# A two-head recurrence on one core: products on half tiles of the matrix array turned into whole-array products

## The chip, the cores and the metric

One core of a Trainium2 chip runs the kernel. The time is device microseconds (us) of one execution; lower is better. A run of a kernel gives one time, and a profiled execution gives the trace from which all rows below are taken. Five engines work side by side, each on a stream of its own: PE (the 128x128 matrix array, with PEld for its weight loads), DVE (vector), ACT (scalar), POOL (GpSimd) and SP (which issues most DMAs). "Fill" is used below for matrix work that depends on no other work at hand.

## The reference, cut to what matters

Two batches of 512 tokens go through one layer: an RWKV-7 branch run in both directions, an attention branch (MLA), gates, an output projection, then a feed-forward block. The change is in the RWKV-7 branch. Per head (8 of them, 64 channels) and direction the recurrence is

```python
def step(state, inp):
    r_t, w_t, k_t, v_t, kk_t, a_t = inp
    sa = jnp.einsum('bhvk,bhk->bhv', state, kk_t)
    state = (state * w_t[:, :, None, :]
             - sa[..., None] * (kk_t * a_t)[:, :, None, :]
             + v_t[..., None] * k_t[:, :, None, :])
    return state, jnp.einsum('bhvk,bhk->bhv', state, r_t)
```

## The kernel before, in words

**Units, chunks and products.** The recurrence is computed in chunks of 64 tokens (`CH`), eight per sequence (`NCH`). A unit is one batch and one pair of heads (4 pairs, 2 batches, 8 units, named `00`, `10`, `01`, ... for batch and pair); head A lies on partitions 0 to 63 (`HA`), head B on 64 to 127 (`HB`), and the two directions are `i` or `d` = 0, 1. `state()` goes through the chunks of one unit. For each chunk PE does, for both directions and both heads:

- s1 (L892, L893): reads the state; K = 128, 64 columns, once into `HA` and once into `HB`. DVE copies the result to `rs` (L895).
- o1 (L904, L906): the part of the output that reads the state, into the bank `o`.
- s2 (L917, L918): the solve, the inverse matrix `e` of the chunk times `rs`; K = 64, one product per head. ACT copies head A's half into `sva` (L919), DVE head B's into `svb` (L920).
- s3 (L925, L926): what the chunk adds to the state; K = 128. DVE adds it to the decayed state `sp` (L927, L928; `sp` is made by POOL, L913, L914).
- o inner (L930, L932): the part of the output inside the chunk, `arb` times `sva`/`svb`; K = 64.

A product of plain f32 appears in the trace as two records, each with a weight load. The shapes in the rows (`128*64`, `64*64`, `128*128`) are the rows and columns of the array that a record uses. All s1, s2 and s3 results share one PSUM buffer (`st`, `NST` = 1).

**Around the recurrence.** `prep()` makes a unit's operands (products `gx`, `gy`; DVE masks them into `nt`, `arb`, `kra`, `krb`; transposes `tb`, `tk`, `vp`, copied out by ACT through `tr_halves`, L641). `lanes()` inverts the 32x32 diagonal blocks on POOL, through DRAM (`nt_d`, `e_d`). `merge()` loads the inverses into `e` (L863), transposes a block (L864, tile `tp`) and joins the blocks by small products `zp` and `xp`. `post()` normalises the output of a unit.

**What sets the order.** Six generators (state, post, merge, prep, fill, combine) are run by `drive()`, which keeps a planned time per thread: a `yield L1` says how much planned time must pass before the thread goes on, and threads are taken in the order of that list. PE instructions keep exactly the order in which `drive()` meets them; the instructions of the other engines are placed by a scheduler. The fill thread supplies the projections `pj_rkv`, `pj_gt`, later the attention (`sc`, `pt`, `pav`, `qps`, `kps`). Those projections are products of 128x128 by 512 in a rounded f32 format. The numbers `L1`, `L2`, `L3` (recurrence), `YT2` (prep's transposes), `YO1` (post) and `YQ` (attention) are such planned times.

Of the kernel before, what the change touches and what calls it, by code (L numbers as in the profile page):

```python
# [41 lines left out]
L1 = 0.7  # L42
L2 = 0.9
L3 = 1.0
# [17 lines left out]
YT2 = 0.8  # L62
YM1 = 2
YM2 = 1.1
YO1 = 1.3
# [3 lines left out]
YQ = 2.6  # L69
# [35 lines left out]
def trunk(ctx, tc, outs, x, w_in, w2, g2, w_uq, w_ukk, w_ukv, w_oab, w_out, w_gu, w_down,  # L105
# [524 lines left out]
    NI = 2  # L630
    HA, HB = slice(0, 64), slice(64, 128)
# [54 lines left out]
    class Unit:  # L686
        count = 0
        first = True

        def __init__(self, b, p):  # L690
            self.b, self.p, self.nm = b, p, f"{b}{p}"
            self.par = Unit.count % 2
            Unit.count += 1
# [4 lines left out]
        def prep(self, free):  # L698
            b, p, nm, tmp = self.b, self.p, self.nm, self.tmp
            kra, krb, arb, bka, bkb = [], [], [], [], []  # L700
# [47 lines left out]
            sva = rp.tile([P, NI, NCH, CH], F32, tag="sva", bufs=2, name=f"sva{nm}")  # L748
            svb = rp.tile([P, NI, NCH, CH], F32, tag="svb", bufs=2, name=f"svb{nm}")
# [4 lines left out]
            for d, (rev, pp_, bt_, kt_) in enumerate(halves):  # L754
# [7 lines left out]
                nt_ = rp.tile([P, NCH, CH], F32, tag="nt", bufs=1, name=f"nt{nm}{d}")  # L762
                rb_ = rp.tile([P, NCH, CH], F32, tag="arb", bufs=4, name=f"arb{nm}{d}")
                for g in range(2):
# [8 lines left out]
                    nc.vector.tensor_mul(nt_[:, gs], gx[:, :, 0:CH], mb[:, :, 0:CH])  # L773
                    nc.vector.tensor_mul(rb_[:, gs], gx[:, :, CH:], mb[:, :, CH:])
                for h, hs in enumerate((HA, HB)):
                    q0 = (d * 2 + h) * NCH
                    nc.sync.dma_start(nt_d[self.par][q0:q0 + NCH].rearrange("c r t -> r c t"), nt_[hs])
# [3 lines left out]
            for d, (rev, pp_, bt_, kt_) in enumerate(halves):  # L781
# [12 lines left out]
                ba_ = rp.tile([P, NCH, CH], F32, tag="bka", bufs=4, name=f"bka{nm}{d}")  # L794
                bb_ = rp.tile([P, NCH, CH], F32, tag="bkb", bufs=4, name=f"bkb{nm}{d}")
# [14 lines left out]
                bka.append(ba_), bkb.append(bb_)  # L810
            self.sva, self.svb, self.pc = sva, svb, pc
            self.kra, self.krb, self.arb, self.bka, self.bkb = kra, krb, arb, bka, bkb

        def lanes(self):
# [15 lines left out]
            for s in range(31):  # L830
                n = 31 - s
                for eng, m0, m1, el in els:
# [3 lines left out]
                    lt = rp.tile([P, 144], F32, tag=f"lt{m0}", bufs=1, name=f"lt{nm}{s}{m0}")  # L836
# [13 lines left out]
        def merge(self):  # L850
# [3 lines left out]
            for i in range(NI):  # L854
                e_ = rp.tile([P, NCH, CH], F32, tag="e", bufs=4, name=f"e{nm}{i}")

                def tmp3(name):
                    return rp.tile([P, NCH, 32], F32, tag=name, bufs=1, name=f"{name}{nm}{i}")
                tp, ntl, z_ = tmp3("tp"), tmp3("ntl"), tmp3("z")
                for h, hs in enumerate((HA, HB)):  # L860
                    q = slice((i * 2 + h) * NCH, (i * 2 + h + 1) * NCH)
                    nc.sync.dma_start(ntl[Q[2 * h]], nt[q, 0:32, 32:].rearrange("c r t -> r c t"))
                    nc.sync.dma_start(e_[hs], ed[q].rearrange("c r t -> r c t"))  # L863
                nc.vector.transpose(tp, e_[:, :, 0:32])  # L864
# [8 lines left out]
                for c in range(NCH):  # L873
                    for h in range(2):
                        mm(xp_[Q[2 * h], c], z_[Q[2 * h + 1], c], e_[Q[2 * h + 1], c, 32:],
                           tile_position=(h * 64 + 32, h * 64))
                yield YM2
                for h in range(2):
                    (nc.scalar.copy, nc.vector.tensor_copy)[h](e_[Q[2 * h], :, 32:], xp_[Q[2 * h], 0:NCH])
                self.ee.append(e_)  # L880

        def state(self):
            nm, sva, svb, pc, ee = self.nm, self.sva, self.svb, self.pc, self.ee
            kra, krb, arb, bka, bkb = self.kra, self.krb, self.arb, self.bka, self.bkb
# [3 lines left out]
               skip_group_check=True)  # L888
            for c in range(NCH):
                s1 = psf.tile([P, NI, CH], F32, tag="st", bufs=NST, name=f"s1{nm}{c}")  # L890
                for i in range(NI):
                    mm(s1[HA, i], kra[i][:, c, 0:CH], sva[:, i, c])  # L892
                    mm(s1[HB, i], krb[i][:, c, 0:CH], svb[:, i, c])  # L893
                rs_ = rp.tile([P, NI, CH], F32, tag="rs", bufs=3, name=f"rs{nm}{c}")
                nc.vector.tensor_copy(rs_, s1)  # L895

                def oslice(i):
                    cn = c if i == 0 else NCH - 1 - c
                    return slice(cn * CH, (cn + 1) * CH)

                def orev(i, t):
                    return t if i == 0 else t[:, ::-1]
                for i in range(NI):
                    mm(op[HA, oslice(i)], sva[:, i, c], orev(i, kra[i][:, c, CH:]), start=False, stop=False,  # L904
                       skip_group_check=True)
                    mm(op[HB, oslice(i)], svb[:, i, c], orev(i, krb[i][:, c, CH:]), start=False, stop=False,  # L906
                       skip_group_check=True)
                last = c == NCH - 1
                yield L1
                if not last:  # L910
                    sp_ = rp.tile([P, NI, CH], F32, tag="rs", bufs=3, name=f"sp{nm}{c}")
# [3 lines left out]
                s2 = psf.tile([P, NI, CH], F32, tag="st", bufs=NST, name=f"s2{nm}{c}")  # L915
# [3 lines left out]
                nc.scalar.copy(sva[HA, :, c], s2[HA])  # L919
                nc.vector.tensor_copy(svb[HB, :, c], s2[HB])  # L920
                yield L2
                if not last:
                    s3 = psf.tile([P, NI, CH], F32, tag="st", bufs=NST, name=f"s3{nm}{c}")
# [3 lines left out]
                    nc.vector.tensor_add(sva[HA, :, c + 1], s3[HA], sp_[HA])  # L927
# [785 lines left out]
```

## Time and profile before

| what | value |
|---|---|
| three runs | 1833.29, 1835.57, 1837.47 us; median 1835.57 |
| the profiled execution | 1835.74 us, span of the trace 1834.0 us |
| mean granted PE clock | 0.978 |
| recurrence (first s1 to last s1) | 278 to 897 us |
| PE, DVE, ACT, POOL busy | 95%, 61%, 42%, 35% of the span |

How to read it: a unit's eight chunks take about 50 us, some 80 us pass from one unit's first chunk to the next one's. Between the chunks' products PE runs fill. A PE record's length is longer than its distance to the next record, since records overlap; so costs on PE are read from starts, not from lengths.

### The profile page before, as it was taken

How to read it: one execution, taken by the hardware profiler on the slowest of the kernel's cores; microseconds unless marked ns; L12 is line 12 of the kernel's file. 1: busy time of each engine (PE TensorE's matmuls, PEld its weight loads, DVE VectorE, ACT ScalarE, POOL GpSimd, SP SyncE). 2: the span in 40 equal slices, each digit the busy share in tenths (PEclk: the TensorE clock that was granted, in tenths of full speed). 3: DMA queues.
4: the chain of work that ended last, by engine and by line, in shares of the span. 5: the costliest groups of instructions: out<-in, count | busy, mean ns of one | idle time of the engine just before them, and what ended most of it. 6: DMA issues, size and time to landing. Idle time of an engine off the chain costs nothing.

```text
span 1834.0 us, 31000 instructions
## 1 busy us (share of the span) xinstructions
PE 1734.3 (95%) x11676; PEld 1365.7 (74%) x11676; DVE 1116.9 (61%) x1957; ACT 771.0 (42%) x1496; POOL 642.2 (35%) x992
## 2 busy tenths in 40 slices
PE   6999999999999998899989999699999999989997
PEld 6887766777677775565657979578888888868886
DVE  6633555635364455877786556865655555588757
ACT  5434343333434334656663233333333333335445
POOL 3012345362635536161112123853434333100006
PEclk8999989999999998999999999899999999999999
DMA  4354433425343334212067551022222222274342
GB/s 163 123 175 163 123 107 82 124 71 136 81 125 106 89 113 119 61 36 55 21 233 249 190 178 35 24 81 93 103 95 84 92 81 92 98 273 134 121 139 92
DMA packets 185333, 208.97 MB, mean 114 GB/s; under 512 B 102816, under 2 KB 114464, under 8 KB 185184
## 3 DMA queue, kind: packets, MB, share of 16 engines
q1 hardware_dynamic: 184320, 205.48, 35.4%
q8 instruction: 92, 1.51, 0.3%
q10 hardware_dynamic: 720, 0.98, 0.2%
q0 software_dynamic: 144, 0.52, 0.1%
q14 instruction: 57, 0.47, 0.1%
HBM read 147.70 MB, written 59.24 MB: 113 GB/s over the span
## 4 chain that ended last, share of the span: by engine, by line
PE 70%; DVE 9%; DMA 8%; POOL 5%; issue 3%; ACT 2%; SPq 1%; DVEq 0%; POOLq 0%; ACTq 0%
PE pgC L125 9%; PE pj_gt L125 8%; PE pgB L125 6%; PE pgA L125 6%; PE pj_rkv L125 5%; PE dx L125 5%; PE dy L125 3%; PE s L125 3%; PE pab L125 2%; PE sc L125 2%; PE pav L125 2%; PE pj_mla L125 2%; DMA wor<-in_w_out 2%; PE o L125 2%; PE gx L125 2%
## 5 line engine op out<-in xcount | busy, mean ns | idle before, releaser
L839 POOL TENSOR_TENSOR lt<-lane,el 128x126 f32<-128x126 f32 (+22 forms) x248 | 93.4, 377 | 38.1 <-DMA lane<-nt_d 19.6
L841 POOL TENSOR_TENSOR el<-el,lt 128x126 f32<-128x126 f32 (+22 forms) x248 | 98.6, 398 | 19.0
L125 PE MATMUL pab<-yo,wab 128*128 128x512 f32 x384 | 94.7, 400 | 5.9 <-ACT yo L132 3.2
L125 PE MATMUL pj_gt<-h_hi,whi_gt 128*128 128x512 f32 x240 | 99.2, 413 | 0.0
L125 PE MATMUL pj_gt<-h_hi,wlo_gt 128*128 128x512 f32 x240 | 98.8, 412 | 0.1
L125 PE MATMUL pj_gt<-h_lo,whi_gt 128*128 128x512 f32 x240 | 98.1, 409 | 0.0
L125 PE MATMUL pwo<-woh,m 128*128 128x256 f32 x512 | 93.8, 283 | 0.1
L125 PEld LDWEIGHTS pab<-yo,wab 128*128 128x128 f32 x384 | 71.9, 191 | 26.0 <-DVE wab L133 4.2
L1203 POOL TENSOR_TENSOR s<-uraw 128x512 f32<-128x512 f32 x22 | 29.3, 1330 | 152.1 <-DMA uraw<-in_w_gu 152.1
L125 PEld LDWEIGHTS pwo<-woh,m 128*128 128x128 f32 x512 | 80.3, 192 | 0.6 <-ACT woh L132 0.3
L125 PE MATMUL pj_rkv<-h_hi,wlo_rkv 128*128 128x512 f32 x192 | 79.7, 418 | 0.0
L125 PE MATMUL pj_rkv<-h_lo,whi_rkv 128*128 128x512 f32 x192 | 79.1, 412 | 0.0
L125 PE MATMUL pj_rkv<-h_hi,whi_rkv 128*128 128x512 f32 x192 | 78.3, 408 | 0.0
L125 PE MATMUL pwo<-wol,m 128*128 128x256 f32 x256 | 72.4, 284 | 0.9 <-DVE wol L133 0.9
L1582 POOL TENSOR_TENSOR x<-x,dp 128x512 f32<-128x512 f32 x4 | 6.3, 1590 | 178.1 <-DVE x L1581 178.1
L1271 DVE TENSOR_TENSOR p<-p,pgC 128x512 f32<-128x512 f32 x22 | 15.1, 687 | 86.9 <-PE pgC L125 86.9
L919 ACT COPY sva<-s 64x128 f32<-64x128 f32 x64 | 16.5, 258 | 104.6 <-PE s L125 96.3
L1050 POOL TENSOR_TENSOR g<-g 128x512 f32<-128x512 f32 x16 | 24.9, 1554 | 92.7 <-DVE g L1048 84.5
L466 POOL TENSOR_SCALAR lut<-lut 128x512 f32<-128x512 f32 x32 | 20.5, 641 | 98.4 <-ACT lut L464 98.1
L125 PEld LDWEIGHTS pj_gt<-h_hi,wlo_gt 128*128 128x128 f32 x240 | 45.1, 188 | 9.5 <-DVE wlo_gt L133 0.8
L125 PEld LDWEIGHTS pj_gt<-h_hi,whi_gt 128*128 128x128 f32 x240 | 45.1, 188 | 8.6
L125 PEld LDWEIGHTS pj_gt<-h_lo,whi_gt 128*128 128x128 f32 x240 | 45.1, 188 | 8.4
(1559 smaller groups left out, 5552.9 us busy)
## 6 DMA issues: line engine op xcount, KB each, us to landing
graw<-in_w_gu SPq DMA_DIRECT2D x22, 512.0 KB, 3.5
uraw<-in_w_gu SPq DMA_DIRECT2D x22, 512.0 KB, 3.5
a_d<-a SPq DMA_DIRECT2D x21, 512.0 KB, 3.3
w<-in_w_down SPq DMA_DIRECT2D x42, 256.0 KB, 4.1
x<-in_x SPq DMA_DIRECT2D x16, 512.0 KB, 8.2
rwkv_in<-lut SPq DMA_DIRECT2D x32, 256.0 KB, 2.0
gate_d<-gtt SPq DMA_DIRECT2D x32, 256.0 KB, 2.5
wab<-in_w_oab SPq DMA_DIRECT2D x32, 256.0 KB, 3.6
```

What stands on the lines that cost most here:

```text
L125: pin(nc.tensor.matmul(out, lhsT, rhs, start=start, stop=stop, **kw), n if out.shape[0] > 64 else n / 2)
L466: nc.gpsimd.tensor_scalar(t, t, f, f, op0=ALU.mult, op1=ALU.add)
L839: eng.tensor_mul(lv, lane[:, s, s + 1:].unsqueeze(1).to_broadcast([P, m_, n]), el[:, 0:m_, s].unsqueeze(2).to_broadcast([P, m_, n]))
L841: eng.tensor_add(ev, ev, lv)
L919: nc.scalar.copy(sva[HA, :, c], s2[HA])
L1050: nc.gpsimd.tensor_add(g_[:, 0], g_[:, 0], g_[:, 1])
L1203: vg(ES[min(j, 1)]).tensor_add(s1, a21, a22)
L1271: nc.vector.tensor_add(p1, p1, x_)
L1582: nc.gpsimd.tensor_add(xs(1, t, 1), xs(1, t, 1), p5[t])
```

## The change

Three things are done to the recurrence.

1. **Solve and state addition on the whole array.** `e` becomes a tile of 128 columns that holds both heads' inverses as two diagonal blocks, zero elsewhere (zeroed once by POOL). One product of K = 128 per direction replaces the two of s2. `bka`/`bkb` become one tile `bk`, `sva`/`svb` halves of one tile `sv`, and s3 is one product 128x128x128 per direction, of whose result only the two diagonal blocks are read.
2. **The inner output product of a chunk moves** from behind that chunk's s3 to behind the next chunk's o1 (`o_inner(c - 1)`); the last chunk's stays where it was.
3. **Room in SBUF**: three `e` tiles (`NEB`) instead of four, which also serve as `nt`; `merge()`'s second direction therefore waits until the state of the unit before is done, since it overwrites that unit's first `e`; `tp` and `z` share a buffer; `rs` has two buffers, not three; `lanes()` writes its intermediate into used rows of `lane`. The mask product into `nt` and the transposes are issued per head (two instructions for one), since the two heads' blocks no longer lie in the same columns.

Five planned times change with it: `L1` 0.7 to 0.57, `L3` 1.0 to 1.06, `YT2` 0.8 to 0.93, `YO1` 1.3 to 1.02, `YQ` 2.6 to 2.89.

```diff
...
+            if not Unit.e:
+                Unit.e = [rp.tile([P, NCH, P], F32, name=f"e{j}") for j in range(NEB)]
+                for t in Unit.e:
+                    for h, hs in enumerate((HA, HB)):
+                        nc.gpsimd.memset(t[hs, :, (1 - h) * CH:(2 - h) * CH], 0.0)
...
-                    nc.vector.tensor_mul(nt_[:, gs], gx[:, :, 0:CH], mb[:, :, 0:CH])
+                    for h, hs in enumerate((HA, HB)):
+                        nc.vector.tensor_mul(nt_[h][:, gs], gx[hs, :, 0:CH], mb[hs, :, 0:CH])
...
+                if i and self.at and NEB < 4:
+                    yield has("state", self.at - 1)
+                e_ = Unit.e[(2 * self.at + i) % NEB]
...
-                nc.vector.transpose(tp, e_[:, :, 0:32])
+                    nc.vector.transpose(tp[Q[2 * h]], eh(h, 0, Q[2 * h]))
...
+                if c:
+                    o_inner(c - 1)
...
                 for i in range(NI):
-                    mm(s2[HA, i], ee[i][HA, c], rs_[HA, i])
-                    mm(s2[HB, i], ee[i][HB, c], rs_[HB, i])
...
+                    mm(s2[:, i, 0:CH], ee[i][:, c], rs_[:, i])
...
                     for i in range(NI):
-                        mm(s3[HA, i], bka[i][:, c], sva[:, i, c])
-                        mm(s3[HB, i], bkb[i][:, c], svb[:, i, c])
...
+                        mm(s3[:, i], bk[i][:, c], sv[:, i, c])
...
-                for i in range(NI):
-                    mm(op[HA, oslice(i)], sva[HA, i, c], orev(i, arb[i][HA, c]), start=False,
-                       stop=False, skip_group_check=True)
-                    mm(op[HB, oslice(i)], svb[HB, i, c], orev(i, arb[i][HB, c]), start=False,
-                       stop=False, skip_group_check=True)
+                if last:
+                    o_inner(c)
                 yield L3
```

How the built program's order changes is shown at three places of unit `02`, the fifth of the eight. In the names, digits behind s1, s2, s3 are the unit and the chunk (`s3023` is s3 of unit 02, chunk 3), and the number behind the underscore is the buffer.

**First place, PE, chunk 3.** Before, s3 and the inner output products of the same chunk stand together, ahead of the gate projection `pj_gt`:

```order
L125 MATMUL s3023_6800<-sva02_5347,bka020_5741 64x64 [waits DVE_49]
L125 MATMUL s3023_6800<-svb02_5348,bkb020_5742 64x64
L125 MATMUL s3023_6800<-sva02_5347,bka021_5915 64x64
L125 MATMUL s3023_6800<-svb02_5348,bkb021_5916 64x64
L125 MATMUL o02_6435<-arb020_5456,sva02_5347 64x64
L125 MATMUL o02_6435<-arb020_5456,svb02_5348 64x64
L125 MATMUL o02_6435<-arb021_5531,sva02_5347 64x64
L125 MATMUL o02_6435<-arb021_5531,svb02_5348 64x64
L125 MATMUL pj_gt600_6817<-h_hi0_137,whi_gt600_6821 128x512
```

Now the chunk begins with s1, o1 and then the inner output products of chunk 2 (the rows with `arb`):

```order
L125 MATMUL s1023_6415<-sv02_5160,kra020_5164 64x64 [waits DVE_49,PE_49]
L125 MATMUL s1023_6415<-sv02_5160,krb020_5165 64x64
L125 MATMUL s1023_6415<-sv02_5160,kra021_5296 64x64
L125 MATMUL s1023_6415<-sv02_5160,krb021_5297 64x64
L125 MATMUL o02_6140<-kra020_5164,sv02_5160 64x64
L125 MATMUL o02_6140<-krb020_5165,sv02_5160 64x64
L125 MATMUL o02_6140<-kra021_5296,sv02_5160 64x64
L125 MATMUL o02_6140<-krb021_5297,sv02_5160 64x64
L125 MATMUL o02_6140<-arb020_5248,sv02_5160 64x64 x2
L125 MATMUL o02_6140<-arb021_5320,sv02_5160 64x64 x2
```

and its s3 is two whole-array products between the prep's transposes `tk` and the projection:

```order
L129 MATMUL tk120_6453<-idn_62,kt120_6045 128x128 x3
L125 MATMUL s3023_6462<-sv02_5160,bk020_5494 128x128 [waits DVE_49]
L125 MATMUL s3023_6462<-sv02_5160,bk021_5670 128x128
L125 MATMUL pj_gt511_6118<-h_hi1_139,whi_gt511_6127 128x512
L125 MATMUL pj_gt511_6118<-h_lo1_140,whi_gt511_6127 128x512
```

Four half-tile products became two whole-array ones, and the half-tile inner products now stand beside other half-tile products.

**Second place, PE, chunk 0.** Before, the solve s2 follows directly on prep's products `gx` of the next unit, which use the array in the same 64x64 tiles:

```order
L125 MATMUL gx1201_6450<-kra120_6321,bt120_6293 64x128
L125 MATMUL gx1201_6450<-krb120_6322,bt120_6293 64x128
L125 MATMUL s2020_6462<-rs020_6442,e020_6210 64x64 [waits DVE_49]
L125 MATMUL s2020_6462<-rs020_6442,e020_6210 64x64
L125 MATMUL s2020_6462<-rs020_6442,e021_6334 64x64 x2
L125 MATMUL pj_gt510_6399<-h_hi0_137,whi_gt510_6403 128x512
```

Now `gx` stands ahead of a whole-array s2:

```order
L125 MATMUL gx1200_6154<-kra120_6069,bt120_6042 64x128
L125 MATMUL gx1200_6154<-krb120_6070,bt120_6042 64x128
L125 MATMUL s2020_6166<-rs020_6147,e2_1715 128x64 [waits DVE_49]
L125 MATMUL s2020_6166<-rs020_6147,e0_1713 128x64 [waits Activation_49]
L125 MATMUL pj_gt510_6117<-h_lo0_138,whi_gt510_6121 128x512
```

The pair keeps its place, but its two groups no longer share a tile shape.

**Third place, ACT, chunk 3.** Before, ACT copies out the transposes `tb` and `tk` of the next unit's prep and makes `kt` for the unit after it, and only then copies the solve's result:

```order
L641 COPY bka120_6710<-tk120_6766 64x4x64 [waits PE_49]
L641 COPY bka120_6710<-tk120_6766 64x4x64
L641 COPY bkb120_6711<-tk120_6766 64x4x64 x2
L743 ACTIVATE kt030_7265<-a030_7255,oka_66,col_60 128x512 [waits DMAHW1_49]
L919 COPY sva02_5347<-s2023_6780 64x2x64 [waits PE_49,Pool_49]
```

Now the copy stands ahead of those of `tk` and of `kt`:

```order
L642 COPY bk120_6399<-tb120_6430 64x4x64 x3
L940 COPY sv02_5160<-s2023_6444 64x2x64 [waits PE_49,Pool_49]
L642 COPY bk120_6399<-tk120_6453 64x4x64 [waits PE_49]
L642 COPY bk120_6399<-tk120_6453 64x4x64 x3
L746 ACTIVATE kt030_6950<-a030_6940,oka_66,col_60 128x512 [waits DMAHW0_49]
```

Five instructions that stood ahead of the copy now stand behind it.

More of the change, by code (lines that the diff above doesn't have):

```diff
@@ L809, in prep @@
                 yield YT2
[L810 to L812 removed]
+                bk.append(bk_)
+            self.sv, self.pc = sv, pc
+            self.kra, self.krb, self.arb, self.bk = kra, krb, arb, bk
         def lanes(self):
```

92 lines of the change are left out of this document (51 added, 41 removed).

## The prediction

> **What bounds the kernel now.** I read the page first, then the busy time by stretches, then the waits of PE inside the recurrence, then the timeline of PE around single products.
>
> ```profile
> span 1834.0 us, 31000 instructions
> ...
> PE 1734.3 (95%) x11676; PEld 1365.7 (74%) x11676; DVE 1116.9 (61%) x1957; ACT 771.0 (42%) x1496; POOL 642.2 (35%) x992
> ```
>
> ```profile
> 600.00:680.00 80.00, 78.97 (x823) 59.06 (x820) 38.26 (x82) 30.73 (x66) 41.24 (x93) 1.00 0.37 103
> ```
>
> ```profile
> PE s L125 <- DVE svb L920: 14.5, 13, 2.8
> ...
> PE s L125 <- DVE rs L895: 2.9, 4, 1.0
> ```
>
> PE is busy 1734.3 of 1834.0 us. The second fence is one unit's 80 us (columns: length, then PE, PEld, DVE, ACT, POOL busy, granted clock, DMA share, GB/s): PE has work for 78.97 of 80 us at full clock, since fill stands between the chunks' products. The recurrence's latency is therefore hidden, and a microsecond counts only if PE spends it in the array or waits. The third fence lists what PE waited for between 278 and 905 us (total, times, longest): 14.5 us for the solve's result ahead of s3, 2.9 us for `rs` ahead of s2. So the change is worth what it saves of array time, plus what it does to these waits.
>
> **Array time: the price of a half-tile group.** What a group costs is the distance between the fill around it, less the fill's own pitch.
>
> ```profile
> 613.91 0.40 PE L125 MATMUL pj_gt<-h_hi,whi_gt 128*128 128x512 f32 x1
> 614.14 0.39 PE L125 MATMUL pj_gt<-h_lo,whi_gt 128*128 128x512 f32 x1
> 614.49 0.45 PE L125 MATMUL s<-rs,e 64*64 64x64 f32 x8
> 614.87 0.50 PE L125 MATMUL pj_gt<-h_hi,wlo_gt 128*128 128x512 f32 x1
> 615.20 0.40 PE L125 MATMUL pj_gt<-h_hi,whi_gt 128*128 128x512 f32 x1
> ```
>
> ```profile
> 625.76 0.22 PE L125 MATMUL s<-sva,kra 128*64 128x64 f32 x1
> ...
> 626.11 0.22 PE L125 MATMUL o<-kra,sva 128*64 128x64 f32 x1
> ...
> 629.66 0.40 PE L125 MATMUL pj_gt<-h_hi,wlo_gt 128*128 128x512 f32 x1
> ...
> 630.23 0.22 PE L125 MATMUL s<-sva,bka 128*64 128x64 f32 x1
> 630.29 0.22 PE L125 MATMUL s<-sva,bka 128*64 128x64 f32 x1
> ...
> 630.45 0.27 PE L125 MATMUL o<-arb,sva 64*64 64x64 f32 x1
> ...
> 630.56 0.22 PE L125 MATMUL o<-arb,sva 64*64 64x64 f32 x1
> ...
> 630.83 0.50 PE L125 MATMUL pj_gt<-h_hi,whi_gt 128*128 128x512 f32 x1
> 631.17 0.40 PE L125 MATMUL pj_gt<-h_lo,whi_gt 128*128 128x512 f32 x1
> ```
>
> Fill starts every 0.23 us (613.91 to 614.14). From 614.14 to 615.20 lie 1.06 us; two pitches of fill taken off leave 0.60 us for s2. Inside a group a pair of records, one per head, takes 0.058 us (six pairs from 625.76 to 626.11, s1 and o1 of one chunk). s2's eight records are four pairs, 0.23 us, so going from whole-array fill into half tiles and back costs 0.60 - 0.23 = 0.37; fill's starts scatter by 0.01, and I use 0.36. Between two half-tile groups of different shape (s3, then o) the last pair is followed after 0.16 us (630.29 to 630.45) and o's first pair after 0.11 (to 630.56): 0.15 more than two pairs, less than half of an in-and-out.
>
> **Array time: the price of a whole-array group.** The trace has no whole-array f32 product of 64 or 128 columns. Its nearest rows are the f32 products `ss_kk` (whole array, 2 columns) and the f32 transposes `tb` (whole array, 128 columns):
>
> ```profile
> 244.08 0.40 PE L125 MATMUL pj_rkv<-h_lo,whi_rkv 128*128 128x512 f32 x1
> 244.32 0.95 PE L125 MATMUL ss_kk<-blk2sb,kksq 128*128 128x2 f32 x8
> 245.13 0.48 PE L125 MATMUL pj_rkv<-h_hi,wlo_rkv 128*128 128x512 f32 x1
> 245.45 0.40 PE L125 MATMUL pj_rkv<-h_hi,whi_rkv 128*128 128x512 f32 x1
> ```
>
> ```profile
> 215.47 0.39 PE L125 MATMUL pj_rkv<-h_lo,whi_rkv 128*128 128x512 f32 x1
> 215.70 0.60 PE L129 MATMUL tb<-idn,bt 128*128 128x128 f32 x4
> 216.05 0.47 PE L125 MATMUL pj_rkv<-h_hi,wlo_rkv 128*128 128x512 f32 x1
> 216.37 0.39 PE L125 MATMUL pj_rkv<-h_hi,whi_rkv 128*128 128x512 f32 x1
> ```
>
> By the same measure eight records of `ss_kk` cost 1.37 - 0.46 = 0.91 us, 0.114 each, and four of `tb` 0.90 - 0.46 = 0.44, 0.110 each, with no price for entering or leaving. That both agree at 2 and at 128 columns says that the weights' load sets the pitch; I take 0.110, the row nearest to s3's 128 columns. From below it can hardly be less; from above it is 0.110 + 0.107 if a record's load and its two passes of 128 columns do not overlap (0.107 is twice 128 of the 512 columns that fill streams in 0.23, less its overhead).
>
> **The sum of the array time.** s2 and s3 are 64 and 56 steps of eight half-tile records, 480 pairs at 0.058 = 27.8 us. They become 120 steps of four whole-array records, 480 at 0.110 = 52.8 us: 25.0 us more. Against that stand the changes of tile shape, which I counted in the two built orders: between whole array and part of it 456 before, 320 now, so 68 fewer in-and-outs at 0.36 = 24.5 us less; between half-tile shapes 108 before, 78 now, 30 at 0.15 = 4.5 less. The sum is 25.0 - 29.0 = -4.0 us. Taken alone a chunk between fill would save more: s2 0.60 to 0.44, s3 with o 1.05 (629.66 to 631.17 less two pitches) to 0.44 + 0.38 for o, together some 0.4. It doesn't come to that, because many groups have prep's half-tile products as neighbours:
>
> ```profile
> 626.83 0.40 PE L125 MATMUL pj_gt<-h_hi,wlo_gt 128*128 128x512 f32 x1
> 627.16 0.32 PE L125 MATMUL gy<-kra,kt 64*64 64x128 f32 x1
> ...
> 628.02 0.45 PE L125 MATMUL s<-rs,e 64*64 64x64 f32 x8
> 628.40 0.50 PE L125 MATMUL pj_gt<-h_hi,whi_gt 128*128 128x512 f32 x1
> 628.73 0.39 PE L125 MATMUL pj_gt<-h_lo,whi_gt 128*128 128x512 f32 x1
> ```
>
> `gy` runs from 627.16 to 628.02 and s2 follows in the same tiles, so the two share one in-and-out: there s2 costs only its four pairs, 0.23 us, and on the whole array 0.44. In the built orders 21 of 64 s2 stood so before and 22 stand so now; s1, which gains from such a neighbour too, had one 21 times and has it 9 times.
>
> The Trainium skill, page "TensorEngine Tiling (Array Packing)", section "Theoretical Speedup", speaks against this change: a product whose rows or columns fit 64 gains up to two times by half tiles, so giving them up would double the groups, to 27.8 us more. The rows bear that out (0.110 against 0.058). Its section "Key Properties" has the other half, that a change of tiling mode drains the array; by the first rule alone the sum would be 1835.7 + 27.8 = 1863.5 us, by both it is near the one above. The first alone gets no chance of its own: the rows from 614.14 to 615.20 show the in-and-out's price, and the change removes 68 of them.
>
> **The waits.** Four of them change.
>
> ```profile
> 621.42 0.82 ACT L743 ACTIVATE kt<-a,oka,col 128x512 f32<-128x512 f32 x1
> 622.27 0.26 ACT L919 COPY sva<-s 64x128 f32<-64x128 f32 x1
> ...
> 622.98 0.27 PE L125 MATMUL s<-sva,bka 128*64 128x64 f32 x1 [0.59 <-DVE svb L920]
> ```
>
> - Ahead of s3: in chunk 3 of five units ACT makes `kt` (0.82 us) before it copies the solve's result, and PE waits, here 0.59 us. The changed order puts the copy first in four of these five: about -3 us with the longest of them. The fill between s2 and s3 stays six products, but s2 no longer leaves half tiles, so s3 comes some 0.2 us sooner after its input; for the 13 waits that is +2.6. Net -0.4.
> - Ahead of s2: o inner now lies between s1 and s2 and gives 0.38 us (630.45 to 630.83) of cover; L1 is shorter, but fill there falls by about one product at most. DVE's `rs` copy stood behind a mask product of `gx` in 13 chunks and does so in 2. I take -2.5 of the 2.9 us.
> - Ahead of the next s1: the same 0.38 us of cover is gone between s3 and s1, with six fill products left (1.38 us). Two DVE additions of 0.28 and 0.295 us follow s3 and have to end; 1.38 covers them unless DVE is busy. I take +1.5; the bounds are 0 and 56 x 0.38 = 21.
> - In `merge()`: two transposes instead of one, and the second direction's wait for the first one's `xp`, because `tp` and `z` share a buffer. I take +0.5, bounded by 8 x 0.44 x 2 = 7.
>
> Together -0.9 us.
>
> **The rest.**
>
> ```profile
> L773 DVE TENSOR_TENSOR nt<-gx,msk 128x256 f32<-128x256 f32 x32 | 13.5, 423 | 24.3 <-PE gx L125 21.3 <-DMA nt_d<-nt 2.5
> ...
> L864 DVE STREAM_TRANSPOSE tp<-e 128x256 f32<-128x256 f32 x16 | 7.0, 436 | 17.0 <-DMA e<-e_d 16.2 <-PE zp L125 0.7
> ```
>
> DVE gets 32 more mask products and 16 more transposes: 64 partitions or 32 are no cheaper per element row, so 32 x 0.423 + 16 x 0.436 = 20.5 us. DVE is busy 38 of a unit's 80 us, which covers them; uncovered they would cost up to 20.5. The wait of `merge()` for the state of the unit before holds two loads of `e` on SP, with the gate stores behind them:
>
> ```profile
> 569.86 0.27 PE L125 MATMUL o<-arb,sva 64*64 64x64 f32 x1
> ...
> 574.91 2.64 SPq L863 DMA_DIRECT2D e<-e_d  x4
> ```
>
> That unit's last product is at 569.86, and the inverses come from POOL only in time for loads at 574.91: the wait has 5 us to spare, and I cost it at nothing; without that cover it would hold `merge()` and the stores by as much as the state is late. Six zero fills on POOL fall before the first chunk, where POOL waits for a DMA. `lanes()` works in place with the same instructions. Fewer buffers for `rs` and `e` add no wait where the order is as it is now. The planned times do nothing but choose this order, which is counted above.
>
> **Sum.** -4.0 - 0.9 = -4.9 us against the profiled execution's 1835.74 (span 1834.0 and 1.74 around it; 0.17 above the median of 1835.57): 1830.8, so 1831.
>
> **Rivals.**
> - *No change, 1836.* The waits eat the array's gain: if s3 keeps its 14.5 us plus 2.6, and s1 waits 3 us, and `merge()` 1, the waits are +4.1 with `rs` gone by only 2.5, rather than -0.9, and -4.0 + 4.1 is nothing. For it: array time itself is a difference of two terms near 27 us, and 0.008 us per record (0.118 instead of 0.110) cancels it too. Against it: the places where `kt` and the masks stood in the way are gone from the order.
> - *Slower, 1845: DVE becomes the one waited for.* Place: the `gx` of chunks 0 and 1, where two `nt` products and one `arb` product (1.26 us) now stand ahead of the state's copies. Price: 32 x 0.423 = 13.5 us if each delays PE, 1831 + 13.5. It decides the sign once more than 4.9 of the 13.5 reach PE. For it: DVE's in-order stream lies in the chain at every chunk. Against: in the changed order `rs` precedes the masks in nearly all chunks, and six fill products follow.
> - *Much slower, 1868: load and stream don't overlap on the whole array.* s2 at 0.110 + 0.053 and s3 at 0.110 + 0.107 add 256 x 0.053 + 224 x 0.107 = 37.5 us. It turns the sign above 0.120 per record (4.9 over 480). Against: `tb` streams 128 columns and still has 0.110.
> - *Much faster, 1817: the whole-array record is cheaper than any such row here.* At the half tiles' 0.058 us for s2's 64 columns and the stream's 0.107 for s3's 128, it is 256 x 0.052 + 224 x 0.003 = 14.0 us less. Against: no whole-array f32 row with weights of its own is under 0.110. The Trainium skill, page "TensorE: Matmul & The Clock Gate", section "Back-to-back issue gap", gives about 81 ns for a sustained pair of load and product of 128 columns. By it 480 x 0.029 = 13.9 us go, an estimate that lands on the same 1817; the rows here are f32 and don't show it.
>
> **How the numbers follow.** My forecast, faster by 0.25% with its own range of 1826 to 1831.8, has 0.45; no change 0.34; the DVE rival 0.13; the two large ones 0.04 each. A difference under 0.2% (3.7 us, 1831.9 to 1839.2) can't be told from none by this measurement. So faster 0.49, same 0.34, slower 0.17. The range runs from 1824 (the array at -6, from an in-and-out of 0.38, waits at -6) to 1842 (half of the DVE rival's price); it leaves out the two large rivals and the upper part of the DVE one.
>
> **What would show it.** In the profile after: s2 and s3 as `128*128` records in groups of four at about 0.11 us; lone s2 at 0.44 instead of 0.60 us, s2 behind `gx` dearer by 0.2; PE's wait for the solve's copy below 14.5 us, for `rs` near 0, for the additions ahead of s1 near 1.5; `e` loads issued within a few us of the lanes' end. It is wrong if a whole-array record takes over 0.12 us, if PE waits more for DVE than before, or if the state of a unit ends after the lanes of the next.

## The result and the profile after

The changed kernel takes 1862.4 us (median of 4 runs, 1858.58 to 1863.79), the kernel before 1835.08: a ratio of 1.0136, 95% interval 1.0120 to 1.0152. It is slower by 25 us by the ratio and by 27 by the medians. I had forecast 1831, with a range up to 1842, so the time lies outside the range and on the other side of no change.

The top of the page of the changed kernel:

```profile
span 1859.9 us, 30104 instructions
...
PE 1743.8 (94%) x11196; PEld 1393.8 (75%) x11196; DVE 1141.1 (61%) x2005; ACT 770.8 (41%) x1496; POOL 645.5 (35%) x998
```

PE has 480 instructions less and is busy 9.5 us more, DVE 24 us more. The span grew by 25.9 us, so most of it is time in which PE waits or runs slowly. What PE waited for between 278 and 905 us (total, times, longest), as shown of before in the prediction:

```profile
PE zp L125 <- DVE tz L876: 9.9, 12, 3.4
PE s L125 <- DVE sv L948: 7.3, 8, 1.7
PE s L125 <- DVE sv L941: 5.9, 9, 1.6
PE kps L125 <- ACT wkh L132: 5.3, 1, 5.3
...
PE s L125 <- DVE rs L922: 1.9, 3, 0.9
...
PE xp L125 <- DVE tz L883: 1.7, 1, 1.7
```

The wait ahead of s3 (L941, the copy of the solve's result) fell from 14.5 to 5.9 us. Ahead of s1 (L948, the second addition) stands 7.3 where 0.7 stood, and a wait is there that before did not have at all: `zp` for `tz`, 9.9 us, with 1.7 more for `xp`. These are the products of `merge()`.

Windows over the recurrence tell where the loss lies. First before, then after; each time up to the end of the fifth unit, and from there to the last transpose of the probabilities (length, then PE, PEld, DVE, ACT, POOL busy, clock, DMA share, GB/s):

```profile
278.00:648.90 370.90, 361.34 (x3739) 267.72 (x3738) 185.01 (x387) 142.72 (x307) 191.11 (x441) 1.00 0.37 101
648.90:963.80 314.90, 287.04 (x2579) 198.67 (x2576) 229.14 (x552) 179.63 (x406) 99.67 (x208) 0.97 0.31 92
```

```profile
275.60:659.00 383.40, 367.17 (x3428) 285.48 (x3427) 197.62 (x416) 142.43 (x305) 190.55 (x438) 0.98 0.36 97
659.00:988.70 329.70, 294.17 (x2409) 212.13 (x2408) 237.52 (x567) 180.06 (x408) 101.32 (x210) 0.96 0.31 89
```

Both parts lost. Behind 989 us the two traces run alike, 25 to 26 us apart. Note how different the parts are: in the first PE is busy 361 of 371 us and DVE half of the time; in the second, where attention takes the fill's place, PE is busy 287 of 315 and DVE 229 of 315. My prediction read one stretch, 600 to 680 us, most of it at the end of the first part, and took it for all eight units.

To compare kernels I use two numbers below. "Early" is how much later than before the fifth unit's last o inner record starts, plus 0.228 us for each fill product that is then still to come beyond before's 138. "Rest" is the difference of the profiled spans less that. After: 659.0 - 648.9 = 10.1, 146 products left make 1.8, early +12.0; 25.9 - 12.0 gives a rest of +13.9. Each is from a single profile: kernels that should agree in their early part differ by up to 5 us, and a profiled execution can lie 4 to 6 us off the median of its kernel's runs (1850.6 against 1855.06 in `e_tz` below, 1841.6 against 1835.97 in `b_mask_lo`). So differences of that size in these two numbers show nothing by themselves.

### The profile page after: what moved, and what is told of

Its sections match the earlier page's. It is cut to its first block, busy times and chain, and to the rows that moved or that the text cites. A ratio compares the mean times of both kernels' runs of the same rounds, so it can differ in the third digit from the quotient of the medians.

```text
span 1859.9 us, 30104 instructions
## 1 busy us (share of the span) xinstructions
PE 1743.8 (94%) x11196; PEld 1393.8 (75%) x11196; DVE 1141.1 (61%) x2005; ACT 770.8 (41%) x1496; POOL 645.5 (35%) x998
## 4 chain that ended last, share of the span: by engine, by line
PE 50%; DVE 10%; DMA 8%; POOL 3%; issue 3%; ACT 2%; SPq 1%; POOLq 0%; DVEq 0%; ACTq 0%
PE pgC L125 10%; PE pgB L125 6%; PE pgA L125 6%; PE pj_gt L125 5%; PE dx L125 4%; PE pab L125 2%; PE dy L125 2%; PE s L125 2%; PE sc L125 2%; PE pav L125 2%; PE dz L125 1%; DMA wor<-in_w_out 1%; PE pwo L125 1%; PE o L125 1%; DMA wab<-in_w_oab 1%
## 5 line engine op out<-in xcount | busy, mean ns | idle before, releaser
L848 POOL TENSOR_TENSOR lane<-lane,el 128x126 f32<-128x126 f32 (+22 forms) x248 | 95.0, 383 | 43.6 <-DMA lane<-nt_d 25.2
L850 POOL TENSOR_TENSOR el<-el,lane 128x126 f32<-128x126 f32 (+22 forms) x248 | 99.1, 400 | 19.2
L940 ACT COPY sv<-s 64x128 f32<-64x128 f32 x64 | 16.5, 258 | 146.6 <-PE s L125 132.1
L941 DVE COPY sv<-s 64x128 f32<-64x128 f32 x64 | 18.9, 295 | 63.6 <-ACT sv L940 37.0
L125 PEld LDWEIGHTS pj_gt<-h_hi,whi_gt 128*128 128x128 f32 x240 | 46.5, 194 | 10.1 <-issue 2.1
```

The costliest lines, as they stand in the source:

```text
L125: pin(nc.tensor.matmul(out, lhsT, rhs, start=start, stop=stop, **kw), n if out.shape[0] > 64 else n / 2)
L848: eng.tensor_mul(lv, lane[:, s, s + 1:].unsqueeze(1).to_broadcast([P, m_, n]), el[:, 0:m_, s].unsqueeze(2).to_broadcast([P, m_, n]))
L850: eng.tensor_add(ev, ev, lv)
L940: nc.scalar.copy(sva[HA, :, c], s2[HA, :, 0:CH])
L941: nc.vector.tensor_copy(svb[HB, :, c], s2[HB, :, 0:CH])
```

## The experiments

### The shared buffer in merge

This is the place ahead of the fifth unit's state, PE first, then DVE (start, length, and in brackets the wait and its releaser):

```profile
593.54 0.69 PE L125 MATMUL xp<-e,tz 32*32 32x32 f32 x32
...
595.88 0.40 PE L125 MATMUL pj_gt<-h_hi,wlo_gt 128*128 128x512 f32 x1
597.37 0.24 PE L125 MATMUL zp<-tz,ntl 32*32 32x32 f32 x2 [1.09 <-DVE tz L876]
597.84 0.69 PE L125 MATMUL zp<-tz,ntl 32*32 32x32 f32 x30 [0.22 <-DVE tz L876]
598.46 0.70 PE L125 MATMUL pj_gt<-h_hi,whi_gt 128*128 128x512 f32 x1
598.96 0.63 PE L125 MATMUL pj_gt<-h_lo,whi_gt 128*128 128x512 f32 x1
...
601.94 0.42 PE L125 MATMUL pj_gt<-h_hi,wlo_gt 128*128 128x512 f32 x1
602.20 0.39 PE L125 MATMUL pj_gt<-h_hi,whi_gt 128*128 128x512 f32 x1
```

```profile
595.08 0.69 DVE L743 SCALAR_TENSOR_TENSOR bt<-nkk,a 128x512 f32<-128x512 f32 x1 [1.36 <-DMA a<-rwkv_in]
595.69 0.69 DVE L766 TENSOR_TENSOR kra<-nkk,pp 128x512 f32<-128x512 f32 x1
596.29 0.68 DVE L767 TENSOR_TENSOR kra<-rkv,pp 128x512 f32<-128x512 f32 x1
596.89 0.89 DVE L876 STREAM_TRANSPOSE tz<-e 32x256 f32<-32x256 f32 x2
```

The first direction's `xp` reads the `tz` buffer until about 594.2. The second direction's transposes may take the buffer only then. In DVE's order three products of the next unit's prep stand ahead of them, and the first of those waits for a load. They run at 596.89 and PE stands. Its loss isn't over when `zp` starts: from 598.46 to 601.94 fill starts every 0.43 us instead of 0.23, which costs 1.6 us more; the granted clock there is 0.50. Four such slow stretches stand behind `zp` waits of the changed kernel (near 350, 517, 598 and 684 us), some 6 us in all.

`e_tz` lets `tz` stand for the whole kernel. The transposes write other partitions than `xp` reads, so they need not wait for it:

```
-                tp = z_ = rp.tile([P, NCH, 32], F32, tag="tz", bufs=1, ...)
+                if not Unit.tz:
+                    Unit.tz = [rp.tile([P, NCH, 32], F32, name="tz")]
+                tp = z_ = Unit.tz[0]
```

> The changed kernel with one standing tz tile in place of a new one per direction: the second direction's transposes then wait only for the readers of the rows that they overwrite, not for the first direction's last product. Theory M (the shared buffer in merge): PE's waits for tz, 9.9 + 1.7 us in the changed kernel's trace, go to under 2, and with them the stretches of halved clock behind four of them (6 us): 1862 - 10 to 17 = 1845 to 1852. Theory A (the whole-array products cost more than planned): no effect of its own, 1859 to 1863. Theory S (the waits of s1 for DVE): the same 1859 to 1863, with the 7.3 us of waits ahead of s1 still there.

Measured: 1855.06 us, 1.0115 (1.0099 to 1.0131), 7 us less than the change by the medians and 4 by the ratios, whose intervals overlap a little. PE no longer waits for `tz` ahead of `zp` at all. Early is -2.2 instead of +12.0: up to the fifth unit this kernel is level with the one before. The time fell by only half of that, and the rest rose from +13.9 to +17.0, so some of what is won early seems to be lost later; 1855 is just above the band that I had given. Clearer is the same edit in a pair that stands in the next section: with s2 and s3 on half tiles the time falls from 1864.82 (1.0152 to 1.0190) to 1853.45 (1.0096 to 1.0130), by 11 us with the intervals apart.

`b_tz` does the reverse, it shares the buffer in the kernel before and splits the transpose:

```
-                tp, ntl, z_ = tmp3("tp"), tmp3("ntl"), tmp3("z")
+                ntl = tmp3("ntl")
+                tp = z_ = tmp3("tz")
...
-                nc.vector.transpose(tp, e_[:, :, 0:32])
+                    nc.vector.transpose(tp[Q[2 * h]], e_[Q[2 * h], :, 0:32])
```

> The kernel before with one thing of the change: tp and z in one buffer, and two transposes of 32 partitions. Theory M: PE waits for tz for some 10 us and the clock falls behind the longer pauses, 1835 + 8 to 17 = 1843 to 1852. Theories A and S: nothing of theirs is in it, 1833 to 1838; what I predicted for this step was +0.5, at most 7.

Measured: 1840.48 us, 1.0045 (1.0028 to 1.0061), some 7 to 8 us slower. The waits of PE between 100 and 1010 us have the new row, and its 6.5 us are nearly the difference:

```profile
PE zp L125 <- DVE tz L865: 6.5, 10, 1.3
```

So the buffer is shown from both sides, at about 7 us (4 to 11 by the single figures): at the low end of the 8 to 17 of my second guess or below it, and far above the 0.5 of the prediction.

### Whole array or half tiles

`e_half` is the changed kernel with s2 and s3 on half tiles, the planner's cost of s3 kept; `e_tz_half` is the same edit on `e_tz`:

```
-                    mm(s2[:, i, 0:CH], ee[i][:, c], rs_[:, i])
+                    mm(s2[HA, i, 0:CH], ee[i][HA, c, 0:CH], rs_[HA, i])
+                    mm(s2[HB, i, 0:CH], ee[i][HB, c, CH:], rs_[HB, i])
...
-                        mm(s3[:, i], bk[i][:, c], sv[:, i, c])
+                        mm(s3[HA, i, 0:CH], bk[i][:, c, 0:CH], sva[:, i, c])
+                        mm(s3[HB, i, CH:], bk[i][:, c, CH:], svb[:, i, c])
```

> The changed kernel with s2 and s3 on half tiles again (the halves of the block-diagonal tiles, eight records each), all else kept, the planner's cost of s3 too. Theory A (the whole-array products are the loss): back by most of the 25 us, 1836 to 1845. Theory M (the loss stands in merge): the array time changes by +2 or so (a lone s2 0.587 instead of 0.457, but 0.23 instead of 0.457 beside gx and gy), 1858 to 1867, and the waits for tz stay near 10 us.

> The changed kernel with one standing tz tile, and s2 and s3 on half tiles. Against 1855 for the standing tile with whole-array products. Theory A (whole-array records, 0.115 us in s2 and 0.13 in s3 instead of 0.11, are part of the remaining loss): 1848 to 1853. Theory N (array time comes out the same either way): 1853 to 1859.

Measured: 1864.82 (1.0171, 1.0152 to 1.0190) against 1862.4, and 1853.45 (1.0113, 1.0096 to 1.0130) against 1855.06. In neither pair are the intervals apart (those of the first just touch, with the half tiles slower). The kind of product isn't the loss, and no clear gain either. The edit moves the rest of the order too, so this bounds the products' worth and doesn't measure it. The changed kernel's own rows do: s2 alone among fill, and s3.

```profile
297.05 0.39 PE L125 MATMUL pj_rkv<-h_hi,wlo_rkv 128*128 128x512 f32 x1
297.27 0.55 PE L125 MATMUL s<-rs,e 128*128 128x64 f32 x4
297.64 0.48 PE L125 MATMUL pj_rkv<-h_hi,whi_rkv 128*128 128x512 f32 x1
297.95 0.39 PE L125 MATMUL pj_rkv<-h_lo,whi_rkv 128*128 128x512 f32 x1
```

```profile
376.42 0.40 PE L125 MATMUL pj_gt<-h_hi,wlo_gt 128*128 128x512 f32 x1
376.65 0.66 PE L125 MATMUL s<-sv,bk 128*128 128x128 f32 x4
377.06 0.48 PE L125 MATMUL pj_gt<-h_hi,whi_gt 128*128 128x512 f32 x1
377.38 0.39 PE L125 MATMUL pj_gt<-h_lo,whi_gt 128*128 128x512 f32 x1
```

s2 costs 0.90 less two pitches of fill, 0.44 here and 0.457 in the median of 24; s3 0.96 less 0.46, 0.50 here and 0.51 in the median of 11. A record is thus 0.114 in s2 and 0.128 in s3, 0.120 over both, against the 0.110 of the sum. The difference is 64 x 0.017 + 56 x 0.07 = 5 us, which alone turns the predicted -4.0 us of array time to +1.

### DVE's extra work, o inner's place, and the planned times

`b_mask` splits the `nt` mask product in the kernel before, everything else keeping its order; `b_mask_hi` does it in units 6 to 8 alone, `b_mask_lo` in units 1 to 5:

```
-                    nc.vector.tensor_mul(nt_[:, gs], gx[:, :, 0:CH], mb[:, :, 0:CH])
+                    for hs in (HA, HB):
+                        nc.vector.tensor_mul(nt_[hs, gs], gx[hs, :, 0:CH], mb[hs, :, 0:CH])
```

> The kernel before with each nt mask product split into two of 64 partitions (32 more DVE instructions of 0.423 us, 13.5 us of DVE time), as in the change; the order of everything else stays. Theory D (DVE's extra work is what the attention stretch pays for, where the changed kernel with a standing tz loses 13 us while up to 680 us it is level with before): 1834 + 5 to 13 = 1839 to 1847, most of it behind 700 us. Theory P (the other order of work in the attention stretch is what costs there): covered, 1833 to 1837.

> The kernel before with the nt mask products split in units 6 to 8 alone (12 more DVE instructions, 5.1 us). Theory D (in the attention stretch DVE's time is nearly all paid for): 1833 + 4 to 7 = 1837 to 1840. Rival, that any disturbance costs whatever its place: about three eighths of the 4.5 us of the full split, 1835.

> The kernel before with the nt mask products split in units 1 to 5 alone (20 more DVE instructions, 8.5 us). Theory D: covered, 1831 to 1834. Rival: five eighths of the 4.5 us, 1836.

Measured: 1837.81 (1.0022, 1.0012 to 1.0032), 1840.12 (1.0024, 1.0014 to 1.0034) and 1835.97 (1.0013, 0.9999 to 1.0027). Five us of DVE's time in the last three units cost 4.4 us (2.6 to 6.2), nearly all of it; 8.5 us in the first five cost 2.4 (-0.2 to 5.0), which fits both theories, and all of it together 4.0 (2.2 to 5.9), no more than the last units' part alone. I had costed all of it at nothing. Yet in the changed kernel taking it away wins nothing. `e_tz_nact` writes `nt` by ACT copies and leaves the mask out:

```
-                        nc.vector.tensor_mul(nt_[h][:, gs], gx[hs, :, 0:CH], mb[hs, :, 0:CH])
+                        nc.scalar.copy(nt_[h][:, gs], gx[hs, :, 0:CH])
```

> The changed kernel with one standing tz tile and nt written by ACT copies, without the mask: DVE loses 64 mask products of 64 partitions (27 us), ACT gets 64 copies; PE's order is the same. Theory D: the late units lose 5 to 10 us less, 1844 to 1850. Theory P (the order of PE there and waits for loads and ACT): 1851 to 1858.

Measured: 1854.18 (1.0102, 1.0081 to 1.0122) against 1855.06. Theory D asked for 1844 to 1850 and isn't borne out: with 25 us less on DVE (1115.8 instead of 1140.6) the time is the same. But ACT has 23 us more in exchange (794.6 instead of 771.3), so what the edit won on DVE could have been lost on ACT; no run parts the two.

`b_o` moves only o inner in the kernel before (`if c: o_inner(c - 1)` behind o1, and `o_inner(c)` behind s3 for the last chunk alone); `b_o4` does so in the first four units only. `e_tz_ob` puts it back behind s3 in `e_tz`; `e_tz_o4` keeps it moved there in the first four units only:

```
-                if c:
+                if c and self.at < 4:
                     o_inner(c - 1)
...
-                if last:
+                if last or self.at >= 4:
                     o_inner(c)
```

> The kernel before with only the o inner products moved from behind s3 to between s1 and s2 of the next chunk. What I predicted for this part: 30 half-half switches kept or lost at 0.15, rs waits 2.5 less, s1 waits 1.5 more: 1830 to 1836. Theory O (taking the 0.38 us of cover from between s3 and s1 is what costs, as the waits of s1 in the changed kernel's trace say, 7 to 9 us): 1840 to 1848.

> The kernel before with o inner moved in the first four units only; the last four keep it behind s3. Theory St (the move pays where fill stands between the products, units 1 to 4, 5.3 us in the trace with the move everywhere, and costs where attention takes the fill's place, units 5 to 8, 15 us there): 1833 - 5 + 0 to 3 = 1827 to 1832. Theory R (the gain in the early units is given back later in any case, since what comes after waits for something else): 1833 to 1838.

> The changed kernel with one standing tz tile and o inner back behind s3; left of the change are the whole-array products, the split masks and transposes on DVE, and the planned times. Theory O+D (of the 21 us that the standing tile leaves, o inner's move makes about 12, as alone in the kernel before, and DVE's extra work 4 to 5): 1841 to 1847. Theory P (the order of the attention stretch, not the move): 1851 to 1858.

> The changed kernel with one standing tz tile and o inner moved in the first four units only. Theory St: units 1 to 5 stay 4 us ahead of before, and units 6 to 8 lose 10 rather than 19 us: 1840 to 1846. Theory P: 1850 to 1856, with units 6 to 8 losing 15 to 19 us as they do with the move everywhere.

Measured: `b_o` 1844.54 (1.0064, 1.0049 to 1.0079), `b_o4` 1843.16 (1.0051, 1.0037 to 1.0065), `e_tz_ob` 1859.47 (1.0138, 1.0121 to 1.0155), `e_tz_o4` 1858.77 (1.0132, 1.0112 to 1.0151). Early, `b_o` is at -3.0 and `b_o4` at -3.5: where fill stands between the products the move may pay, as predicted, but 3 us are within what profiles differ by. Both lose 11.5 us in the rest, though in `b_o4` o inner stands in its old place there. So it isn't the move as such, and my theory of stages (St) falls: what costs is something that any of these edits changes in the last units. Putting o inner back in `e_tz` didn't help either, in the last four units or in all.

That something could be the order. `e_times` and `e_tz_yt` give the changed kernel and `e_tz` planned times of before (all five, and YT2 alone); `e_arr` is `e_tz_ob` with all five (their lines drawn together here):

```
-L1 = 0.57 / L3 = 1.06 / YT2 = 0.93 / YO1 = 1.02 / YQ = 2.89
+L1 = 0.7  / L3 = 1.0  / YT2 = 0.8  / YO1 = 1.3  / YQ = 2.6
```

> The changed kernel with the planned times of before (L1 0.7, L3 1.0, YT2 0.8, YO1 1.3, YQ 2.6). Theory T (these five times, chosen for another order, make the waits): 1840 to 1852. Theories M and A: the waits move about but their sum stays, 1856 to 1868. L1 at 0.7 gives s2 more fill ahead of it, L3 at 1.0 takes a little from s1: the wait ahead of s1 at 7 to 10 us.

> The changed kernel with one standing tz tile and YT2 back at 0.8, which alone of the five planned times moves much of the order. Theory P (the remaining 13 to 20 us are the new order in the attention stretch): 1840 to 1850, with the gain behind 700 us. Theories D and O (DVE's extra work, or the moved o inner): 1852 to 1860.

> Of the change only the block-diagonal tiles and the whole-array products (with their masks, transposes and the standing tz tile): o inner behind s3 and the five planned times of before. If the products and DVE's extra work are all that it costs: 1833 + 4.5 + 0 to 4 = 1837 to 1842. If the order that the planner makes of any edit costs in the attention stretch: 1845 to 1860, as with the other planned times (1859).

Measured: `e_times` 1863.67 (1.0165, 1.0146 to 1.0185), `e_tz_yt` 1847.35 (1.0078, 1.0060 to 1.0097), `e_arr` 1877.96 (1.0237, 1.0217 to 1.0256). So the planned times of before don't bring the time back by themselves: `e_times` is where the change was, and `e_arr` lies above both bands that I had given. But one of them does much in `e_tz`: YT2 alone wins 7.7 us, with the intervals of `e_tz_yt` and `e_tz` just apart. `e_arr` and `e_tz_ob` hold the same work and differ in five numbers of the plan, and 18 us lie between them. An order is worth that much. In the traces `e_arr` waits 10.2 us ahead of `xp` for `tz`, `e_tz_ob` 1.5, and PE's granted clock up to the fifth unit's end is 0.97 against 1.00.

The last three change one planned time of attention in `e_tz`, so that the order is the same up to about 715 us: PL 3.5 to 4.5 (`e_tz_pl`), YK 1.8 to 2.6 (`e_tz_yk`), YA1 0.5 to 0.8 (`e_tz_ya`).

> The changed kernel with one standing tz tile and attention's planned time from scores to the next product at 4.5 instead of 3.5: the order is the same until about 715 us, behind that the transposes of the probabilities come later. Theory P (the loss of the last three units is the order in the attention stretch, in which products come before their inputs): units 1 to 5 end as in the standing-tile kernel, and the time moves by more than 4 us, to 1842 to 1851 if the products came too early. Rival (the late units lose to something that no order mends): 1853 to 1857.

> The changed kernel with one standing tz tile and attention's planned time behind the keys at 2.6 instead of 1.8; same order until about 715 us. Theory P: 1842 to 1851, or a loss of the same size; the rival: 1853 to 1857.

> The changed kernel with one standing tz tile and the first of attention's planned times at 0.8 instead of 0.5; same order until about 715 us. Theory P: 1842 to 1851, or a loss of the same size; the rival: 1853 to 1857.

Measured: 1855.51 (1.0109, 1.0092 to 1.0126), 1851.39 (1.0091, 1.0072 to 1.0110) and 1849.67 (1.0074, 1.0048 to 1.0100), against 1.0115 (1.0099 to 1.0131) for `e_tz`. One doesn't move, the second's interval overlaps, and the third is about 5 us lower, with intervals that just touch. With `e_tz_yt` this shows the order as a part of the loss, of 5 to 8 us, and doesn't show it for all.

| kernel | early, us | rest, us |
|---|---|---|
| changed | +12.0 | +13.9 |
| e_tz | -2.2 | +17.0 |
| e_half | +8.3 | +20.2 |
| e_tz_half | +0.5 | +19.6 |
| e_tz_ob | +4.3 | +16.4 |
| e_tz_o4 | +0.5 | +26.1 |
| e_times | +15.8 | +12.1 |
| e_tz_yt | -0.4 | +14.5 |
| e_tz_nact | +0.5 | +21.4 |
| e_tz_pl | +2.6 | +23.1 |
| e_tz_yk | -1.0 | +18.5 |
| e_tz_ya | +0.4 | +13.6 |
| e_arr | +22.4 | +24.6 |
| b_tz | +5.6 | -3.5 |
| b_o | -3.0 | +11.5 |
| b_o4 | -3.5 | +11.5 |
| b_mask | -1.9 | +6.5 |
| b_mask_hi | -1.6 | +6.9 |
| b_mask_lo | -0.4 | +6.2 |

The last column parts the kernels in two. `b_tz` and the three `b_mask` keep PE's order of before; their rest is -3.5 to +6.9. All others have another order on PE; theirs is +11.5 or more, and in `b_o` and `b_o4` the other order is all that differs.

### What the last three units wait for

The waits of PE from the end of the fifth unit to the last transpose, of before and of `e_tz`, of which these lead:

```profile
PE s L125 <- DVE svb L920: 8.0, 5, 2.8
PE pt L129 <- DVE pr L610: 5.3, 3, 4.2
PE kps L125 <- ACT wkh L132: 3.5, 1, 3.5
```

```profile
PE pt L129 <- DVE pr L610: 6.8, 6, 3.4
PE kps L125 <- ACT wkh L132: 6.5, 1, 6.5
PE s L125 <- DVE sv L944: 5.9, 8, 1.9
PE s L125 <- DVE sv L951: 3.9, 3, 1.8
...
PE pt L129 <- DVE qf L539: 2.0, 1, 2.0
```

All rows together are 27.7 us in 23 waits before and 41.2 in 37 in `e_tz`: 13.5 us more, of the 17 that the rest lost. They are many, and none has more than 4 us of it. The clock isn't it: the granted clock is 0.97 there in both. One can be followed to its end, attention's entry, where `kps` waits 3.5 us before and 6.5 in `e_tz`. On ACT stand, in `e_tz`:

```profile
711.32 0.26 ACT L943 COPY sv<-s 64x128 f32<-64x128 f32 x1 [4.68 <-PE s L125]
711.34 0.33 ACTq L482 DMA_DIRECT2D pq<-mla_d  x1
711.77 0.40 ACTq L514 DMA_DIRECT2D wk<-in_w_ukk  x1
...
716.87 0.62 ACT L132 CAST lat<-pq 128x512 fp32r<-128x512 f32 x1 [3.55 <-DMA pq<-mla_d]
717.31 0.33 ACTq L482 DMA_DIRECT2D pq<-mla_d  x1
717.39 0.29 ACT L132 CAST wkh<-wk 128x128 fp32r<-128x128 f32 x1
```

ACT's queue holds the second load of `pq` behind the recurrence's copy, which waits 4.68 us for s2; the load lands late, the cast of `wkh` stands behind it, and PE has no fill left. In the kernel before the same copy ran at 707.33 and let both loads go at 707.35, ahead of the last fill products.

## Why the prediction was wrong, point by point

Two steps failed above all. The term for `merge()` was put at 0.5 us and cost about 7. And the order of the work outside the recurrence was put at nothing, while the last three units lost 14 to 17 us. The first is shown; for the second the rows are shown, and the cause in part.

- **Merge, the term of the sum that was mis-sized most.** I took +0.5 us for "the second direction's wait for the first one's `xp`", with a bound of 7. It measured 9.9 + 1.7 us of waits, some 6 of slowed fill behind them, and 7 us in the time when taken out. The bound counted the transposes' own 0.44 us. What had to be counted was what stands in DVE's order ahead of them: at four of the seven places where `zp` waits, the ones with the slow stretches, it is the three products of the next unit named above, whose first waits up to 2.9 us for its load; at the others it is different work.
- **One unit read for eight.** "The recurrence's latency is therefore hidden" is true of the 80 us shown. In the last three units PE was busy 287 of 315 us, and of them only the first 31 us stand in that window. There every kernel in the table whose PE order differs from before's lost 11 to 26 us.
- **"The planned times do nothing but choose this order, which is counted above."** I counted the order's tile shapes and four waits, in the recurrence alone. Attention's entry, its transposes and its softmax weren't counted, and their waits grew by more than the recurrence gained. `b_o` prices a change of order by itself: of the change it has the move of o inner alone, which I had put among the gains, and it is 9 to 14 us slower than before.
- **DVE's extra work at nothing.** In the kernel before its masks cost 4 us, and those of the last three units alone as much. The DVE rival looked for it at the `gx` of chunks 0 and 1 of every unit.
- **The wait ahead of s1.** +1.5 was predicted, and it went from 0.7 to 7.3 us. One of them, on DVE and on PE:

```profile
556.68 0.69 DVE L801 TENSOR_TENSOR kra<-gy,msk 64x512 f32<-64x512 f32 x1
557.39 0.68 DVE L802 TENSOR_TENSOR krb<-gy,msk 64x512 f32<-64x512 f32 x1
558.00 0.27 DVE L947 TENSOR_TENSOR sv<-s,sp 64x128 f32<-64x128 f32 x1
558.28 0.29 DVE L948 TENSOR_TENSOR sv<-s,sp 64x128 f32<-64x128 f32 x1
```

```profile
557.27 0.50 PE L125 MATMUL pj_gt<-h_hi,wlo_gt 128*128 128x512 f32 x1
558.73 0.24 PE L125 MATMUL s<-sv,kra 128*64 128x64 f32 x1 [0.96 <-DVE sv L948]
```

  `gy`'s masks run on DVE ahead of the additions, and PE waits 0.96 us for the second. I had taken six fill products as cover there, "unless DVE is busy". Here DVE was, and two fill products and eight pairs of `gy` stood between s3 and s1.
- **Array time.** s3's record is 0.128, not 0.110; the -4.0 us were about +1. The two kinds of product came out even: 0.120 over both is the point at which, by the prediction, the sign turns. The two large rivals (0.163 or more a record, and 0.058) did not occur. By the estimate from the page "TensorEngine Tiling (Array Packing)" of the Trainium skill, section "Theoretical Speedup", the time would have been 1863.5, almost what was measured; but half tiles brought back nothing (1864.82), so that near hit is chance.
- **Right.** The wait ahead of s3 fell to 5.9 us by the copy's new place. A lone s2 is 0.457 us for the 0.44 predicted. PE's work held up the `e` loads by 1.0 us at the seventh unit and by 0.5 us or less elsewhere, so that the wait for the state cost little. The 5 us to spare were read at one unit, though: even in the kernel before, the seventh unit's loads start at 733.69, ahead of the sixth unit's last product at 736.8.
- **Not decided.** Five eighths of my -4.9 us, -3.1, fall on the first five units. With the shared buffer put out of the way `e_tz` has -2.2 there, but four kernels with its order up to there have -1.0 to +2.6, so neither -3.1 nor nothing is shown.

What stays open is the loss of the last three units, 14 to 17 us. Shown are its rows (13.5 us of waits in `e_tz`) and that neither o inner's place nor the kind of product makes it in the changed kernel; DVE's masks don't either, unless ACT's copies cost as much. That it is the order is supported by `b_o` and `b_o4` (the same work as before in another order, 11.5 us in the rest), by `e_tz_yt` (7.7 us back) and by `e_arr` against `e_tz_ob`. No order was found that gives it all back, and no version here beats the kernel before.

## What to carry to other kernels

Read every stage that a change touches, the ones with thin cover first: a table of windows over the whole run, rather than one busy unit, would have shown where a wait can't hide. When two tiles are made to share a buffer, price the wait by what is queued ahead of the waiting instruction on its engine, not by that instruction's length. And where a planner orders the work, an edit's own cost comes with that of a new order, which can be several times larger; run the same work under two orders before you ascribe the difference to the work.

## What the runs showed of the hardware that I had not expected

PE's clock was halved after quite short pauses. After 1.1 us of waiting and 1.1 us of 32x32 products, fill ran at a start every 0.43 us for 3.5 us (598.46 to 601.94, granted clock 0.50) and then at 0.23 again. The Trainium skill, page "TensorE: Matmul & The Clock Gate", Part 1, tells of half rate after an idle window of about 3.4 us and of full rate after as long a busy one. The length of the slow stretch and the halving agree with the trace; the pause ahead of it was a third of that window. The pause's length alone doesn't decide it. Between 278 and 700 us the changed kernel has seven waits of over 0.9 us: the four ahead of `zp` (0.97 to 3.37 us) and one of 1.68 us ahead of s1 (at 641.58) have a slow stretch behind them, one of 0.96 ahead of s1 (at 558.73) and one of 1.01 ahead of s3 have none. In `e_tz` none of four has one, though the longest is 2.0 us, and in `b_tz` one of three ahead of `zp` has. What does decide it, no run here shows.
